# Gate vectors computed with tokens on the partitions, and an input norm with all token loads ahead and one scaling per tile

## The chip, the cores and the metric

The kernel runs on 1 core of one Trainium2 chip. The metric is the device time of one execution in microseconds (us). The kernel before took 2186.8, 2188.89 and 2193.44 us in three runs, median 2188.89 us.

A core has five engines with their own instruction streams: TensorE (PE in the profile, with its weight loads as PEld), VectorE (DVE), ScalarE (ACT), GpSimd (POOL) and SyncE (SP), which here only starts DMAs. Each engine works through its stream in order and waits on semaphores that other engines and DMAs raise.

## The reference, cut to what matters

The program is one inference step of a two-layer trunk: a gated DeltaNet layer and an RWKV-7 layer, over 8 x 8 sample tokens, 16 learned meta tokens and 1024 prompt tokens, 1104 rows of 1024 values in all. The change touches the start of the first layer: the RMSNorm of its input, and two small vectors for each token and each of 16 heads, `beta` and `g`, with the running sums of `g` that the chunked delta rule needs.

```python
def rmsnorm(x, w):
    xf = x.astype(jnp.float32)
    return xf * lax.rsqrt(jnp.mean(xf * xf, -1, keepdims=True) + RMS_EPS) * w.astype(jnp.float32)
...
proj = xn @ w_in
qkv, z, b, a = proj[..., :c1], proj[..., c1:c2], proj[..., c2:c3], proj[..., c3:]
beta = jax.nn.sigmoid(b)
g = -jnp.exp(a_log.astype(jnp.float32)) * jax.nn.softplus(a + dt_bias)
...
gc = jnp.cumsum(g, axis=-1)                      # within a chunk
decay = jnp.exp(jnp.where(causal, gc[..., :, None] - gc[..., None, :], -jnp.inf))
g_last = gc[..., -1]
k_dec = k * jnp.exp(g_last[..., None] - gc)[..., None]
q_dec = q * jnp.exp(gc)[..., None]
S = S * jnp.exp(gl_c)[..., None, None] + ...
```

The kernel cuts the 1104 rows into 9 token tiles: tile 0 holds the 64 sample tokens (8 chunks of 8 rows), the 16 meta tokens and 48 prompt tokens, tiles 1 to 7 hold 128 prompt tokens each and tile 8 the last 80. So the running sums restart every 8 rows in the first 64, at row 64, and at the start of every tile after that.

## The kernel before, in words

**Input.** `input_load` (L272) makes one tile `x` of 128 tokens by 1024 values for each of the 9 token tiles and loads it through SP's queue; tile 0 comes in three pieces, and the norm's weight is loaded once as `nwb`, the same row on all partitions. `build` (L2116) calls it for tiles 0 to 2 first; `layer0` (L2132) calls `gates_open`, which issues the loads of the gate weights `wz` (two DMAs of 16 columns out of a wide matrix) and of the two per-head constants `al`, and after it `input_load` for tiles 3 to 8.

`input_norm` (L280) works in groups of tiles, [0,1], [2,3,4], [5,6], [7,8]. For each tile ACT squares it with a running sum (`junk`, `ss`); then DVE, POOL (a power of -0.5, L103) and DVE (a Newton step, L111 to L113) turn the sums of a group into `rs`. Six of the tiles are scaled by `rs` and `nwb` in one DVE instruction (L299). The other three, 3, 5 and 7, are multiplied by `nwb` on POOL (L291) and by `rs` on ACT. Then PE transposes the tile in two halves of four 128x128 blocks into PSUM tiles named `r` (three buffers) and `f` (two buffers), ACT copies each half rounded to `xh` (tiles `xa`, `xc`), and DVE stores what was rounded off as `xl` (three instructions for each token tile, L313). Every later product of the layer uses the pair.

**Gates.** `gates_open` (L317) and the generator `gates` (L346) keep heads on the partitions and tokens along the free dimension: 16 partitions of 1104 tokens. `gates` projects with 64 columns of weights (three products named `d`, of 24 matmuls each, one for each segment of 384, 384 and 336 tokens), takes tanh, adds the bias, takes exp for each segment, then on all 1104 tokens at once log (ACT), max and add (L370), a multiply (L371), a running sum with restarts (L373, the one scan), and differences to the end of the chunk (L379 to L382). ACT takes the exp of the chunk ends (`egl`), which goes out to DRAM and comes back on all 128 partitions as `eglb`; the running sums themselves go to DRAM as `drow` in eight DMAs. Then nine PE transposes of 96 rows of `rows` give a form with tokens on the partitions, from which DVE and ACT fill `gcol`: beta, minus the sum, exp of the sum, exp of the distance to the end.

**Order.** From `layer0`'s products on, the order on PE and ACT is written by hand: each product of 128 output columns (`k`, `q`, `v`, `w`) takes six slots of 12 matmuls each, numbered from -24, and `gdn_events` (L921) puts other steps at fractions of slots; the five stages of `gates` stand at -22.9, -19.4, -16.8, -16.7 and -16.6 (L928). A product's PSUM tile is `dk`, `dq` or `dv`; its weights come as `wraw`, are split by ACT (`whi`, L87) and POOL (`wlo`, L91), half a product at a time. On DVE, POOL and SP, and on all engines in what lies ahead of the products, a list scheduler sets the order.

**What follows the gates.** For key head pair 0, `decays` (L643) reads `drow` back on all partitions as `E`, POOL masks it, ACT takes exps with `gcol` as bias, PE forms key scores `fsc`, DVE scales them (L700 to L710), they pass through DRAM to a blocked form `invA`, DVE inverts 72 triangular blocks in 31 dependent steps (L571, L573), and the result returns through DRAM as `T1n`, which PE's merges (`rY`) read. `history_turn` (L477) is one transpose, `mhist`, just ahead of the products' main part.

## Time and profile before

| | |
|---|---|
| runs | 2186.8, 2188.89, 2193.44 us; median 2188.89 us |
| the profiled execution's own time | 2190.08 us |
| its span, first to last instruction | 2188.3 us |
| granted TensorE clock, mean | 0.981 |
| PE busy | 2048.3 us, 94% |
| DVE busy | 1585.8 us, 72% |
| ACT busy | 1290.9 us, 59% |
| POOL busy | 841.2 us, 38% |

A row of the timeline reads: start, duration, engine, line, operation, output <- inputs, count, and in brackets how long the engine had been idle ahead of it and what released it. A row of the windows reads: the stretch, its length, then busy time and count for PE, PEld, DVE, ACT and POOL, the granted clock, the DMA engines' busy share, and GB/s. Matmuls overlap in the pipe, so what counts is the distance from one start to the next. SPq is SyncE's queue of DMA issues.

### The profile page before, as it was taken

To read this page: it belongs to the slowest core of one execution; us is meant where nothing else is said; L and a number is where in the kernel's file an instruction comes from. 1 tells how busy PE (TensorE), PEld (TensorE's weight loads), DVE (VectorE), ACT (ScalarE), POOL (GpSimd) and SP (SyncE) were. 2 spreads that over 40 slices of the span, in tenths; PEclk is the share of its full clock that TensorE was granted. 3 is DMA by queue.
4 is the path that set the end of the run, shared out by engine and by line. 5 is a ranking of instruction groups with operands and counts; after the bars stand their busy time and mean duration, and the time that the engine had idled before them with its cause. 6 is when DMAs were issued, how large, how long until landed. Compare 5 with 4: busy or idle time off the path is not lost. (4 is left out here: it accounts for less than half of the span.)

```text
span 2188.3 us, 54818 instructions
## 1 busy us (share of the span) xinstructions
PE 2048.3 (94%) x20404; PEld 1905.8 (87%) x20404; DVE 1585.8 (72%) x4221; ACT 1290.9 (59%) x3761; POOL 841.2 (38%) x1125
## 2 busy tenths in 40 slices
PE   5869899999999999999999999999898999999997
PEld 5859899999999999998899999888898988888876
DVE  7967869788887979795334676757968657777755
ACT  5526466656565665656533365664746446777774
POOL 3423333334343333334231352343534344444444
PEclk9979999999999999999999999999999999999999
DMA  4423342424333333335345115655565476677764
GB/s 119 119 58 87 90 115 85 116 78 106 96 96 106 105 96 102 98 102 165 97 126 134 61 51 190 215 167 168 168 180 152 119 221 175 181 229 221 239 178 138
DMA packets 430661, 292.65 MB, mean 134 GB/s; under 512 B 147145, under 2 KB 412986, under 8 KB 430394
## 3 DMA queue, kind: packets, MB, share of 16 engines
q1 hardware_dynamic: 430394, 289.14, 46.0%
q8 instruction: 161, 2.64, 0.5%
q14 instruction: 106, 0.87, 0.1%
HBM read 197.68 MB, written 91.37 MB: 132 GB/s over the span
## 5 line engine op out<-in xcount | busy, mean ns | idle before, releaser
L91 POOL TENSOR_TENSOR wlo<-wraw,whi 128x512 fp32r<-128x512 f32 (+1 forms) x246 | 328.5, 1337 | 475.8 <-ACT whi L87 432.1
L77 PE MATMUL d<-xc,whi 128*128 128x384 f32 (+2 forms) x1006 | 279.1, 336 | 0.8 <-DVE xc L313 0.7
L524 DVE SCALAR_TENSOR_TENSOR cvy<-raw,cw,cvy 128x408 f32<-128x408 f32 (+2 forms) x288 | 189.1, 657 | 19.2 <-ACT cvy L63 17.8
L87 ACT CAST whi<-wraw 128x512 fp32r<-128x512 f32 (+1 forms) x246 | 149.9, 612 | 87.2 <-PE d L77 50.0
L77 PEld LDWEIGHTS d<-xc,whi 128*128 128x128 f32 (+1 forms) x1006 | 183.0, 189 | 3.4 <-DVE xc L313 1.1
L77 PE MATMUL d<-xc,wlo 128*128 128x384 f32 (+3 forms) x476 | 157.5, 339 | 3.8 <-POOL wlo L91 3.8
L77 PE MATMUL dz<-xc,whi 128*128 128x384 f32 (+1 forms) x480 | 153.7, 338 | 0.0
L77 PE MATMUL dv<-xc,whi 128*128 128x384 f32 (+1 forms) x480 | 152.2, 337 | 0.0
L77 PE MATMUL d<-xa,whi 128*128 128x384 f32 (+3 forms) x450 | 142.9, 341 | 8.4 <-ACT ev L2352 4.1
L63 ACT ACTIVATE o<-rA,gcol 128x128 f32<-128x128 f32 x128 | 42.2, 367 | 116.2 <-DVE S L903 116.0
L571 DVE TENSOR_TENSOR invtmp<-invA,invT 72x31 f32<-72x31 f32 (+15 forms) x248 | 101.8, 411 | 3.2
L77 PE MATMUL dv<-xa,whi 128*128 128x384 f32 (+1 forms) x288 | 99.0, 344 | 0.0
L77 PE MATMUL dz<-xa,whi 128*128 128x384 f32 (+1 forms) x288 | 98.5, 342 | 0.0
L77 PEld LDWEIGHTS d<-xc,wlo 128*128 128x128 f32 (+1 forms) x476 | 89.2, 189 | 7.9 <-POOL wlo L91 4.9
L77 PEld LDWEIGHTS d<-xa,whi 128*128 128x128 f32 (+1 forms) x450 | 84.3, 190 | 12.9 <-ACT ev L2352 4.4
L573 DVE TENSOR_TENSOR invT<-invT,invtmp 72x31 f32<-72x31 f32 (+15 forms) x248 | 92.7, 374 | 3.3
L77 PEld LDWEIGHTS dz<-xc,whi 128*128 128x128 f32 x480 | 89.3, 188 | 4.6 <-issue 4.5
L77 PEld LDWEIGHTS dv<-xc,whi 128*128 128x128 f32 x480 | 89.1, 188 | 1.4 <-issue 1.4
L77 PE MATMUL d<-xa,wlo 128*128 128x384 f32 (+3 forms) x252 | 84.8, 337 | 2.0 <-POOL wlo L91 2.0
L77 PE MATMUL dq<-xc,whi 128*128 128x384 f32 (+1 forms) x240 | 78.3, 343 | 3.0 <-ACT whi L87 3.0
L77 PE MATMUL dk<-xc,whi 128*128 128x384 f32 (+1 forms) x240 | 78.2, 346 | 0.0
L1333 DVE SCALAR_TENSOR_TENSOR mixs<-xb,pcol,mixs 128x320 f32<-128x320 f32 (+2 forms) x96 | 69.4, 733 | 5.0 <-ACT mixs L63 4.7
(523 smaller groups left out, 6821.9 us busy)
## 6 DMA issues: line engine op xcount, KB each, us to landing
wraw<-in_gdn_w_in SPq DMA_DIRECT2D x96, 256.0 KB
wraw<-in_rwkv_w_rkvz SPq DMA_DIRECT2D x80, 256.0 KB
Sb<-in_state_gdn SPq DMA_DIRECT2D x64, 256.0 KB
sldcak<-cakd SPq DMA_DIRECT2D x24, 576.0 KB
wraw<-in_rwkv_w_o SPq DMA_DIRECT2D x42, 256.0 KB
E<-drow SPq DMA_DIRECT2D x24, 384.0 KB
attn<-drow SPq DMA_DIRECT2D x24, 384.0 KB
wraw<-in_gdn_w_out SPq DMA_DIRECT2D x36, 256.0 KB
```

Source lines behind the costliest of these rows:

```text
L63: return self.nc.scalar.activation(out, in_, func, bias=bias, scale=scale, **kw)
L77: self.nc.tensor.matmul(out, lhsT, rhs, start=start, stop=stop)
L87: nc.scalar.copy(hi, x)
L91: e.tensor_tensor(lo, x, hi.bitcast(F32), op=ALU.subtract)
L524: nc.vector.scalar_tensor_tensor(y[0][:, 0:wd], raw[:, k:k + wd], cw[k], y[0][:, 0:wd], op0=ALU.mult, op1=ALU.add)
L571: nc.vector.tensor_tensor(tmp, A[:, j, j + 1:32].unsqueeze(2).broadcast_to([nb, n, m]), Tv[:, j, 0:m].unsqueeze(1).broadcast_to([nb, n, m] ...
L573: nc.vector.tensor_tensor(Tv[:, j + 1:32, 0:m], Tv[:, j + 1:32, 0:m], tmp, op=ALU.subtract)
L1333: nc.vector.scalar_tensor_tensor(x[:, f:], xb[:, 8 + a + f:8 + b], mu, x[:, f:], op0=ALU.mult, op1=ALU.add)
```

## The change

Four things change.

1. `layer0` calls `input_load` for tiles 3 to 8 ahead of `gates_open`.
2. `input_norm` scales all nine tiles in one DVE instruction each; the POOL multiply and the ACT scaling are gone. The second half of tiles 2, 5 and 8 is transposed into PSUM tile `m` and no longer into `f`, and the transposes are issued at high priority.
3. The gates put tokens on the partitions. Each segment's product is copied to `rows` (48 partitions) by one ACT instruction; nine transposes of 48 rows bring everything into one PSUM tile `fgt`; from there on each instruction works on 128 partitions of 9 x 16 values. The running sums, the distances to the chunk's end, and the chunk ends on all partitions are products of PE with 0/1 masks (`upto`, `past`, `part`, built by POOL at the start), into `fgc` and `mge`; the scan, the differences and the DRAM round trip of `eglb` are gone. Two transposes (`fgr`) bring the sums back to rows for `drow`, whose layout stays, in two DMAs in place of eight.
4. The five stages of `gates` become four, at -23.4, -21.4 and -20.4 after the first.

The diff, cut:

```diff
@@ -287,23 +287,19 @@
...
-                if q not in (0,1,2,4,6,8):
-                    nc.gpsimd.tensor_tensor(x[0:nr], x[0:nr], self.nwb[0:nr], op=ALU.mult)
             nc.vector.tensor_scalar(ss, ss, 1.0 / D, RMS_EPS, op0=ALU.mult, op1=ALU.add)
             rs = t(lp, [128, len(qs)], "rs", 2)
             self.rsqrt(rs, ss, lp, "rn")
             for u, q in enumerate(qs):
                 x, nr = self.xrows[q]
                 r = rs[0:nr, u:u + 1]
-                if q in (0,1,2,4,6,8):
-                    nc.vector.scalar_tensor_tensor(x[0:nr], x[0:nr], r, self.nwb[0:nr], op0=ALU.mult, op1=ALU.mult)
-                else:
-                    self.act(x[0:nr], x[0:nr], AF.Identity, scale=r)
+                nc.vector.scalar_tensor_tensor(x[0:nr], x[0:nr], r, self.nwb[0:nr], op0=ALU.mult, op1=ALU.mult)
...
                 for h in (0, 1):
-                    p = self.ps("f", 2) if h else self.ps("r", 3)
-                    for k in range(4):
-                        self.transpose(p[:, 128 * k:128 * k + nr], x[0:nr, 512 * h + 128 * k:512 * h + 128 * k + 128])
+                    p = (self.ps("m", 1) if q % 3 == 2 else self.ps("f", 2)) if h else self.ps("r", 3)
+                    with self.tc.high_priority():
+                        for k in range(4):
+                            self.transpose(p[:, 128 * k:128 * k + nr], x[0:nr, 512 * h + 128 * k:512 * h + 128 * k + 128])
...
@@ -315,93 +311,99 @@
     def gates_open(self, ctx):
...
         gp = self.gatep = ctx.enter_context(self.tc.tile_pool(name="gates", bufs=1, reuse_waits="tile"))
...
-        al = t(gp, [128, 2], "al")
+        al = t(gp, [128, 2, 16], "al")
         wz = t(gp, [128, 8, 64], "wz")
...
         nc.sync.dma_start(wz[:, :, 0:16], wv[:, :, 0:16])
         nc.sync.dma_start(wz[:, :, 32:48], wv[:, :, 16:32])
-        rows = t(gp, [96, 1152], "rows")
...
-        nc.sync.dma_start(al[32:48, 0:1], i["gdn_a_log"].rearrange("l h -> h l"))
-        nc.sync.dma_start(al[32:48, 1:2], i["gdn_dt_bias"].rearrange("l h -> h l"))
+        for x, nm in enumerate(("gdn_a_log", "gdn_dt_bias")):
+            nc.sync.dma_start(al[:, x], i[nm].broadcast_to([128, 16]))
+        rows = t(gp, [48, 1152], "rows")
+        nc.gpsimd.memset(rows[:, NT:1152], NEG)
+        upto, past = [t(gp, [128, 128], f"upto{k}") for k in (0, 1)], [t(gp, [128, 128], f"past{k}") for k in (0, 1)]
+        for k in (0, 1):
+            for m, c, b in ((upto[k], 1, 0), (past[k], -1, -1)):
+                nc.gpsimd.memset(m, 1.0)
+                nc.gpsimd.affine_select(m, m, pattern=[[c, 128]], compare_op=ALU.is_ge, fill=0.0, base=b, channel_multiplier=-c)
+        nc.gpsimd.memset(upto[0][0:64, 64:128], 0.0)
+        nc.gpsimd.memset(past[0][64:128, 0:64], 0.0)
+        part = t(gp, [128, 9], "part")
+        nc.gpsimd.memset(part, 0.0)
+        nc.gpsimd.tensor_copy(part[0:64, 0:8], self.bmask[0:64])
+        nc.gpsimd.memset(part[64:128, 8:9], 1.0)
+        for m, c, b in ((upto[0], 1, 0), (past[0], -1, 7)):
+            v = m[0:64, 0:64].rearrange("p (b r) -> p b r", r=8)
+            nc.gpsimd.affine_select(v, v, pattern=[[-8 * c, 8], [0, 8]], compare_op=ALU.is_ge, fill=0.0, base=b, channel_multiplier=c)
+        self.gate_in = al, wz, rows, upto, past, part
     def gates(self, xh, xl):
         nc, i, t, gp = self.nc, self.i, self.t, self.gatep
-        al, wz, rows, g, sm = self.gate_in
-        nea = t(gp, [128, 1], "nea")
-        self.act(nea[32:48], al[32:48, 0:1], AF.Exp)
-        nc.vector.tensor_scalar(nea[32:48], nea[32:48], -1.0, None, op0=ALU.mult)
+        al, wz, rows, upto, past, part = self.gate_in
+        nea = t(gp, [128, 16], "nea")
+        self.act(nea, al[:, 0], AF.Exp)
+        nc.vector.tensor_scalar(nea, nea, -1.0, None, op0=ALU.mult)
...
         for s, (c0, n) in enumerate(SEGS):
             p = self.dense(w, 64, xh, xl, s)
-            b = rows[0:16, c0:c0 + n]
-            self.act(b, p[0:16, 0:n], AF.Tanh, scale=0.5)
-            nc.vector.tensor_scalar(b, b, 0.5, 0.5, op0=ALU.mult, op1=ALU.add)
...
-            self.act(xa, p[32:48, 0:n], AF.Identity, bias=al[32:48, 1:2])
-            nc.vector.scalar_tensor_tensor(ya, xa, -1.0, xa, op0=ALU.mult, op1=ALU.max)
-            self.act(ya, ya, AF.Exp, scale=-1.0)
+            nc.scalar.copy(rows[:, c0:c0 + n], p[0:48, 0:n])
         yield
...
-        self.act(ya, ya, AF.Ln, bias=1.0)
-        nc.vector.scalar_tensor_tensor(ya, xa, 0.0, ya, op0=ALU.max, op1=ALU.add)
-        nc.vector.tensor_scalar(g[32:48, 0:NT], ya, nea[32:48], None, op0=ALU.mult)
-        gc = rows[32:48]
-        nc.vector.tensor_tensor_scan(gc, sm[32:48], g[32:48], 0.0, op0=ALU.mult, op1=ALU.add)
+        col = self.col
+        p = self.ps("f", 2, "gt")
+        for k in range(9):
+            self.transpose(p[:, 48 * k:48 * k + 48], rows[:, 128 * k:128 * k + 128])
+        pv = p[:, 0:432].rearrange("p (k x) -> p k x", x=48)
+        b, x, y, g = [t(gp, [128, 9, 16], n) for n in ("gb", "gx", "gy", "g")]
+        nc.vector.tensor_tensor(x, pv[:, :, 32:48], al[:, 1].unsqueeze(1).broadcast_to([128, 9, 16]), op=ALU.add)
+        nc.vector.scalar_tensor_tensor(y, x, -1.0, x, op0=ALU.mult, op1=ALU.max)
+        self.act(y, y, AF.Exp, scale=-1.0)
+        self.act(b, pv[:, :, 0:16], AF.Tanh, scale=0.5)
+        self.act(y, y, AF.Ln, bias=1.0)
+        nc.vector.scalar_tensor_tensor(y, x, 0.0, y, op0=ALU.max, op1=ALU.add)
+        nc.vector.tensor_tensor(g, y, nea.unsqueeze(1).broadcast_to([128, 9, 16]), op=ALU.mult)
+        gs = t(gp, [128, 9, 16], "gs")
+        nc.vector.tensor_tensor(gs, g[:, 0].unsqueeze(1).broadcast_to([128, 9, 16]), part.unsqueeze(2).broadcast_to([128, 9, 16]), op=ALU.mult)
+        nc.vector.tensor_scalar(col[:, :, 0, :], b, 0.5, 0.5, op0=ALU.mult, op1=ALU.add)
         yield
...
-        nc.vector.tensor_tensor(c3(gd)[:, 1:9], v[:, 1:9, 127:128].broadcast_to([16, 8, 128]), v[:, 1:9], op=ALU.subtract)
...
-        nc.vector.tensor_tensor(c8(gd), v8[:, :, 7:8].broadcast_to([16, 8, 8]), v8, op=ALU.subtract)
-        egl = t(gp, [48, 17], "egl")
...
-        nc.sync.dma_start(dgl, egl[32:48])
...
+        flat = lambda a: a.rearrange("p k h -> p (k h)")
+        p = self.ps("f", 2, "gc")
+        for a, m in ((0, upto), (144, past)):
+            self.mm(p[:, a:a + 16], m[0], g[:, 0])
+            self.mm(p[:, a + 16:a + 144], m[1], flat(g[:, 1:9]))
+        c, d = (p[:, a:a + 144].rearrange("p (k h) -> p k h", h=16) for a in (0, 144))
+        gc = t(gp, [128, 144], "gc")
+        nc.vector.tensor_copy(gc.rearrange("p (j k h) -> p k j h", j=8, h=2), c.rearrange("p k (j h) -> p k j h", h=2))
+        e = self.ps("m", 1, "ge")
+        self.mm(e[:, 0:144], self.ones, flat(gs))
+        self.mm(e[:, 144:272], self.ones, flat(g[:, 1:9]))
+        self.act(col[:, :, 1, :], c, AF.Identity, scale=-1.0)
+        self.act(self.eglb.rearrange("p h c -> p c h"), e[:, 0:272].rearrange("p (c h) -> p c h", h=16), AF.Exp)
+        self.act(col[:, :, 2, :], c, AF.Exp)
+        self.act(col[:, :, 3, :], d, AF.Exp)
+        yield
+        p = self.ps("f", 2, "gr")
+        self.transpose(p[:, 0:128], gc[:, 0:128])
+        self.transpose(p[0:16, 128:256], gc[:, 128:144])
+        r = t(gp, [128, 256], "gr")
+        nc.vector.tensor_copy(r[:, 0:128], p[:, 0:128])
+        nc.vector.tensor_copy(r[0:16, 128:256], p[0:16, 128:256])
         self.drow = self.dram([8, 9, 2, 128], "drow")
-        for j in range(8):
-            nc.sync.dma_start(self.drow[j].rearrange("t h k -> h t k"), c3(gc)[2 * j:2 * j + 2])
-        for t3 in range(3):
-            yield
-            p = self.ps("f", 2)
-            for k in range(3):
-                self.transpose(p[:, 96 * k:96 * k + 96], rows[:, (3 * t3 + k) * 128:(3 * t3 + k + 1) * 128])
-            pv = p[:, 0:288].rearrange("p (k x h) -> p k x h", k=3, h=16)
-            c = self.col[:, 3 * t3:3 * t3 + 3]
-            nc.vector.tensor_copy(c[:, :, 0, :], pv[:, :, 0, :])
-            nc.vector.tensor_scalar(c[:, :, 1, :], pv[:, :, 2, :], -1.0, None, op0=ALU.mult)
-            self.act(c[:, :, 2, :], pv[:, :, 2, :], AF.Exp)
-            self.act(c[:, :, 3, :], pv[:, :, 4, :], AF.Exp)
+        d = self.drow.rearrange("j t h k -> (j t h) k")
+        nc.sync.dma_start(d[0:128], r[:, 0:128])
+        nc.sync.dma_start(d[128:144], r[0:16, 128:256])
...
@@ -925,7 +927,7 @@
...
-        for u in (-22.9, -19.4, -16.8, -16.7, -16.6):
+        for u in (-23.4, -21.4, -20.4):
             self.at(u, gate)
...
@@ -2138,8 +2140,8 @@
...
         self.gdn_keep(ctx)
         gates = ExitStack()
+        self.input_load(range(3, 9))
         self.gates_open(gates)
-        self.input_load(range(3, 9))
         self.input_norm(hi, lo)
...
```

How the order moves. First **SP's queue** at the program's start: `x_3`, `x_4` and the later `x` are token tiles, `wz` the gate weights, `al` the two constants, `wraw` the first key weights. Before:

```order
L278 DMA nwb_62<-in_norm_w 128x1024
L264 DMA x_3_64<-in_x_prompt 128x1024
L264 DMA x_4_66<-in_x_prompt 128x1024
L332 DMA wz_132<-in_gdn_w_in 128x8x16
L333 DMA wz_132<-in_gdn_w_in 128x8x16
L343 DMA al_131<-in_gdn_a_log 16x1
L344 DMA al_131<-in_gdn_dt_bias 16x1
L264 DMA x_23_146<-in_x_prompt 128x1024
L264 DMA x_24_148<-in_x_prompt 128x1024
```

After:

```order
L264 DMA x_4_66<-in_x_prompt 128x1024
L264 DMA x_15_123<-in_x_prompt 128x1024
L264 DMA x_16_125<-in_x_prompt 128x1024
L264 DMA x_17_127<-in_x_prompt 128x1024
L264 DMA x_18_129<-in_x_prompt 128x1024
L264 DMA x_19_131<-in_x_prompt 128x1024
L264 DMA x_20_133<-in_x_prompt 80x1024
L327 DMA wz_144<-in_gdn_w_in 128x8x16
L328 DMA wz_144<-in_gdn_w_in 128x8x16
L330 DMA al_143<-in_gdn_a_log 128x16
L330 DMA al_143<-in_gdn_dt_bias 128x16
L428 DMA wraw_371<-in_gdn_w_in 128x4x128
```

The six token tiles pass ahead of the gate weights and constants, and the constants come as 128 rows of 16 values.

Second, **DVE** between the end of the input norm and the first key rows: `cvy` is the key product's convolution, `rows`, `ay`, `g` the old gates on 16 partitions, the names with `g` behind them the new ones. Before:

```order
L370 SCALAR_TENSOR_TENSOR ay_413<-ax_412,ay_413 16x1104
L524 SCALAR_TENSOR_TENSOR cvy_565<-raw_524,cw_393,cvy_565 128x408
L371 TENSOR_SCALAR g_138<-ay_413,nea_405 16x1104
L373 SCALAR_TENSOR_TENSOR rows_136<-sm_140,g_138 16x1152
L524 SCALAR_TENSOR_TENSOR cvy_602<-raw_570,cw_393,cvy_602 128x384
L379 TENSOR_TENSOR rows_136<-rows_136 16x1024
L380 TENSOR_TENSOR rows_136<-rows_136 16x64
```

After:

```order
L370 TENSOR_TENSOR gx_554<-fgt_543,al_143 128x144
L371 SCALAR_TENSOR_TENSOR gy_555<-gx_554 128x144
L379 TENSOR_SCALAR gcol_135<-gb_553 128x9x16
L375 SCALAR_TENSOR_TENSOR gy_555<-gx_554,gy_555 128x144
L376 TENSOR_TENSOR g_556<-gy_555,nea_416 128x144
L378 TENSOR_TENSOR gs_564<-g_556,part_166 128x144
L526 SCALAR_TENSOR_TENSOR cvy_582<-raw_521,cw_404,cvy_582 128x408 x3
L388 COPY gc_611<-fgc_606 128x9x8x2
L401 COPY gr_641<-fgr_638 128x128
L402 COPY gr_641<-fgr_638 16x128
```

The gate steps now stand in one block ahead of the convolution, and each has 144 values to a partition, not 1104.

Third, **PE** in the key and query products: before, the gate transposes (`rows`) stand between the first and the second segment of the query product `dq`:

```order
L77 MATMUL dq_699<-xc_107,whi_626 128x384
L74 MATMUL f_726<-ident_74,rows_136 128x96 x3
L74 MATMUL f_734<-ident_74,rows_136 128x96 x3
L74 MATMUL f_742<-ident_74,rows_136 128x96 x3
L77 MATMUL dq_762<-xa_103,whi_585 128x384
```

After, the transposes `fgt` stand around `mhist`, and the mask products in the middle of the second key segment:

```order
L77 MATMUL d_475<-xc_107,whi_86_419 64x336
L74 MATMUL mhist_506<-ident_74,hist_501 128x96
L74 MATMUL fgt_543<-ident_74,rows_150 128x48 x3
L77 MATMUL dk_524<-xc_107,whi_379 128x384
L77 MATMUL dk_524<-xc_107,wlo_380 128x384
```

```order
L77 MATMUL dk_589<-xc_107,whi_375 128x384
L77 MATMUL fgc_606<-g_556,upto_27_152 128x16
L77 MATMUL fgc_606<-g_556,upto_28_153 128x128
L77 MATMUL fgc_606<-g_556,past_29_154 128x16
L77 MATMUL fgc_606<-g_556,past_30_155 128x128
L77 MATMUL mge_613<-gs_564,ones_82 128x144
L77 MATMUL mge_613<-g_556,ones_82 128x128
L77 MATMUL dk_589<-xc_107,whi_379 128x384
```

The two transposes `fgr` follow 12 matmuls later, at the end of that segment. The order on PE from the second query segment on is unchanged.

More of the change, by code (lines that the diff above doesn't have):

```diff
@@ L317, in gates_open @@
     def gates_open(self, ctx):
-        nc, i = self.nc, self.i
+        nc, i, t = self.nc, self.i, self.t
         W = i["gdn_w_in"][0]
-        self.col = self.t(self.l0, [128, 9, 4, 16], "gcol")
-        self.eglb = self.t(self.l0, [128, 16, 17], "eglb")
-        self.bmask4 = self.t(self.l0, [64, 4], "bmask4")
+        self.col = t(self.l0, [128, 9, 4, 16], "gcol")
+        self.eglb = t(self.l0, [128, 16, 17], "eglb")
+        self.bmask4 = t(self.l0, [64, 4], "bmask4")
         for g in (0, 1):
@@ L385, in gates @@
-        self.act(egl[32:48, 8:17].unsqueeze(2), v[:, :, 127:128], AF.Exp)
-        dgl = self.dram([16, 17], "dgl")
-        nc.sync.dma_start(dgl, egl[32:48])
-        nc.sync.dma_start(self.eglb.rearrange("p h c -> p (h c)"),
-                          dgl.rearrange("(o h) c -> o (h c)", o=1).broadcast_to([128, 272]))
-        self.drow = self.dram([8, 9, 2, 128], "drow")
-        for j in range(8):
-            nc.sync.dma_start(self.drow[j].rearrange("t h k -> h t k"), c3(gc)[2 * j:2 * j + 2])
```

20 lines of the change are left out of this document (removed).

## The prediction

> **What bounds the kernel now.** I began with the page's busy shares and then cut the span into windows, because the change touches only the first 75 us or so. PE is busy 94% of the span, and the 40 slices of the page show the first slice and a few others as the gaps. The windows around the start:
>
> ```profile
> 61.80:71.86 10.06, 5.84 (x22) 4.99 (x22) 9.19 (x19) 3.91 (x13) 3.60 (x9) 0.66 0.43 102
> 71.86:118.00 46.14, 43.83 (x321) 41.62 (x319) 44.14 (x127) 25.07 (x71) 22.05 (x37) 1.00 0.43 119
> 118.00:141.30 23.30, 2.96 (x18) 2.72 (x18) 18.04 (x47) 2.82 (x10) 4.39 (x5) 0.66 0.19 47
> 141.30:2188.00 2046.70, 1956.28 (x19813) 1822.05 (x19813) 1469.72 (x3956) 1222.92 (x3607) 788.84 (x1036) 0.99 0.47 136
> ```
>
> From 71.86 to 118 DVE is busy 44.1 of 46.1 us, and from 118 to 141.3 PE does next to nothing. The PE timeline names what it waits for:
>
> ```profile
> 141.32 0.31 PE L77 MATMUL rY<-T1n,E 32*32 32x32 f32 x2 [20.04 <-DMA T1n<-g_t]
> ```
>
> T1n is the end of one chain: gates, decays, key scores, then 31 dependent inversion steps on DVE, then DRAM. So up to 141 us the end is set by when DVE can begin the scores, not by PE's own work, and after it PE is busy 1956 of 2047 us in an order that the change leaves alone. Time won ahead of the scores passes through the 20 us wait to the end one for one; time won on PE alone, with T1n no earlier, would vanish in that wait. I therefore price the change at one point: the start of the second query segment on PE, 71.86 us, after which PE's order is the same and the scores follow at once.
>
> **What stands ahead of 71.86.** PE's rows in the query product:
>
> ```profile
> 61.46 0.33 PE L77 MATMUL dq<-xa,wlo 128*128 128x384 f32 x1
> 61.63 0.34 PE L77 MATMUL dq<-xc,whi 128*128 128x384 f32 x1
> 64.99 0.69 PE L77 MATMUL dq<-xc,whi 128*128 128x384 f32 x1 [3.02 <-ACT whi L87]
> ...
> 70.11 1.05 PE L74 MATMUL f<-ident,rows 96*128 96x96 f32 x6
> 71.61 0.47 PE L74 MATMUL f<-ident,rows 96*128 96x96 f32 x3 [0.46 <-ACT gcol L63]
> 71.86 0.42 PE L77 MATMUL dq<-xa,whi 128*128 128x384 f32 x1
> ```
>
> Starts are 0.17 us apart at full pace. After the 3.02 us wait the last 12 matmuls of the segment take from 64.99 to 70.11, 5.1 us where 12 x 0.175 = 2.1 would do, at a granted clock of 0.66 in that window. The weights `whi` were late because ACT, in order, sat on a convolution that DVE had not finished:
>
> ```profile
> 63.89 0.54 ACT L63 ACTIVATE raw<-cvy 128x408 f32<-128x408 f32 x1 [4.74 <-DVE cvy L524]
> ```
>
> and DVE had not finished it because the old gates stand between its taps:
>
> ```profile
> 55.63 1.30 DVE L370 SCALAR_TENSOR_TENSOR ay<-ax,ay 16x1104 f32<-16x1104 f32 x1 [3.61 <-ACT ay L63]
> 56.96 1.62 DVE L524 SCALAR_TENSOR_TENSOR cvy<-raw,cw,cvy 128x408 f32<-128x408 f32 x1
> 58.62 0.78 DVE L371 TENSOR_SCALAR g<-ay,nea 16x1104 f32<-16x1104 f32 x1
> 59.43 0.64 DVE L524 SCALAR_TENSOR_TENSOR cvy<-raw,cw,cvy 128x408 f32<-128x408 f32 x1
> 60.10 2.55 DVE L373 TENSOR_TENSOR_SCAN rows<-sm,g 16x1152 f32<-16x1152 f32 x1
> ```
>
> **Part 1, the gates: 5.4 us won.** I count from the transpose `mhist`, which stands near the same place in both orders.
>
> ```profile
> 50.29 0.25 PE L74 MATMUL mhist<-ident,hist 96*128 96x96 f32 x1
> ```
>
> Before, `mhist` to 71.86 is 21.6 us. After, PE has behind `mhist`: the wait for the third segment's copy to `rows` (0.45, as ACT's old copies, which were 16 wide, took 0.44 to 0.48) and three `fgt` transposes (0.35); 60 key matmuls, 36 x 0.175 + 24 x 0.155 = 10.0; six mask products; two `fgr` transposes, 0.2; 24 query matmuls, 4.2. The old kernel ran nothing like the mask products; the nearest row is
>
> ```profile
> 74.04 0.83 PE L77 MATMUL fsc<-K 128*128 128x128 f32 x6
> ```
>
> 0.14 each, so 0.7 for four full and two narrow ones (0.3 to 0.9 as bounds, all at a few tenths). With `mhist` itself that is 16.2 us; 21.6 - 16.2 = 5.4. It is the removed stall and slow stretch (6.8) less some more PE work (1.4).
>
> This holds only if no new stall comes. PE reaches the mask products 24 key matmuls, 4.2 us, behind the last `fgt`. In that time DVE must do four small steps, ACT two, with a table load between:
>
> ```profile
> 53.08 1.28 ACT L63 ACT_TABLE_LOAD   x1
> 54.38 1.22 ACT L63 ACTIVATE ay<-ay,cvals 16x1104 f32<-16x1104 f32 x1
> ```
>
> Steps of 144 values are not in the trace; `y`'s old step of 1104 values took 1.30 (L370 above) and steps of two or three values 0.16 (L112 below), so about 0.3 each, and 0.1 for each hand-over: 4 x 0.3 + 3 x 0.3 on ACT + 1.28 + 0.3 = 3.7 us, against 4.2. From below it is 3.0, from above, with 0.5 for each of the seven, 5.1: a stall between nothing and 0.9. I take none. The cover is the key product itself. In the trace the activation behind the load starts 0.02 us after it ends. The Trainium skill, ScalarE: Activation LUTs, section What ACT_TABLE_LOAD costs, puts about 1.38 us of drain on top of each load; by that the chain would be 5.1 us, PE would wait 0.9 and the sum would be 0.9 smaller. The two rows above show no such drain, so I stay with 3.7.
>
> The mask tiles on POOL (some 15 small memsets and selects at 0.1 to 0.3) end by about 7.5 us, ahead of POOL's first norm step, which needs the second square sum, so nothing. The eight `drow` DMAs and the `eglb` round trip leave SP; the two new DMAs leave at about 54, and `E` can be read back some two microseconds later. POOL's mask and DVE's use of `E` in the old trace:
>
> ```profile
> 71.14 0.87 POOL L651 TENSOR_SCALAR_AFFINE_SELECT E<-E 128x768 f32<-128x768 f32 x1
> ```
>
> ```profile
> 78.88 1.64 DVE L710 SCALAR_TENSOR_TENSOR E<-fsc,bp,E 128x128 f32<-128x128 f32 x6
> ```
>
> POOL had `E` by 71.1 and DVE needed it, after ACT's exps, at 78.9; those take some 3 us, so there are about 4 us of room, and `E` moves by about as much as PE. I cost it at nothing; if the room is used up, T1n is late one for one.
>
> **Part 2, the input norm and the load order: 3.8 us won at `mhist`.** SP spent 4.45 us on issuing one of the constants, so the fourth tile was issued at 11.4 and ACT waited for it:
>
> ```profile
> 6.45 4.45 SPq L343 DMA_DIRECT2D al<-in_gdn_a_log  x1
> ...
> 9.92 1.06 ACT L63 ACTIVATE junk<-x 128x1024 bf16<-128x1024 f32 x1 [1.33 <-DMA x<-in_x_prompt]
> ...
> 15.12 1.06 ACT L63 ACTIVATE junk<-x 128x1024 bf16<-128x1024 f32 x1 [1.75 <-DMA x<-in_x_prompt]
> ```
>
> In between, DVE and not the loads is the limit: it is busy nearly throughout 20 to 40 us. A piece of it:
>
> ```profile
> 19.71 2.30 DVE L111 TENSOR_TENSOR rn_t<-rs 128x3 f32<-128x3 f32 x1 [0.33 <-POOL rs L103]
> 22.05 0.16 DVE L112 SCALAR_TENSOR_TENSOR rn_t<-rn_t,ss 128x3 f32<-128x3 f32 x1
> 22.24 0.16 DVE L113 SCALAR_TENSOR_TENSOR rs<-rn_t,rs 128x3 f32<-128x3 f32 x1
> 22.44 2.48 DVE L299 SCALAR_TENSOR_TENSOR x<-x,rs,nwb 128x1024 f32<-128x1024 f32 x2
> 24.84 0.68 DVE L313 TENSOR_TENSOR xc<-r,xa 128x512 fp32r<-128x512 f32 x1
> 25.44 0.41 DVE L313 TENSOR_TENSOR xa<-f,xc 128x256 fp32r<-128x256 f32 x1
> 25.77 0.41 DVE L313 TENSOR_TENSOR xc<-f,xc 128x256 fp32r<-128x256 f32 x1
> ```
>
> L111 is a 0.16 us step; it took 2.30 because a POOL multiply ran beside it:
>
> ```profile
> L291 POOL TENSOR_TENSOR x<-x,nwb 128x1024 f32<-128x1024 f32 x3 | 7.1, 2372 | 1.1 <-ACT junk L63 1.1
> ```
>
> Two of the three multiplies cost DVE some 2.1 us each that way, the third 0.7: 5.0 in all, against three more scalings of 1.24 = 3.7. DVE's work from the first scaling on: nine scalings, 11.2; nine sets of three subtractions, from start to start 0.60 and 0.33 in these rows and 0.33 for the third, at 1.26 (the last tile less), 10.9; four groups of sums and Newton steps at 0.7, 2.8; the parameter columns, 0.7: 25.6. To this come 1.7 us without work while the second group's sums are made, and 2.5 where POOL's splits of the gate and key weights still run beside DVE. The first scaling comes at 11.5, since with the second tile no longer behind the gate weights ACT need not wait the 1.33 us. 11.5 + 25.6 + 1.7 + 2.5 = 41.3, against the old end of the last subtraction:
>
> ```profile
> 45.27 0.32 DVE L313 TENSOR_TENSOR xc<-f,xc 128x160 fp32r<-128x160 f32 x1
> ```
>
> 45.6, so DVE is 4.3 us earlier. PE's part behind the last transposes (the third gate segment, 12 key matmuls, eleven small transposes) is about 7.2 us, and puts `mhist` at about 46.5: 3.8 won. Bounds: if DVE gains nothing from POOL's absence and pays three scalings, -3.7; with no POOL beside it at all and no idle time, +7.
>
> **Part 3, the score steps: 0.8 won.** Before, ACT's copies into `gcol` stand just ahead of the query segment's first tap and delay it; the taps delay the first score on DVE. They are gone from there. Nothing to 1.8 us; I take 0.8.
>
> **The sum.** 5.4 + 3.8 + 0.8 = 10.0 us of the profiled execution's 2190.1, which gives 2180.1. The median of the three runs shown is 1.2 lower, so a median of 2179 to 2180; I say 2180. A measurement of this kernel can tell about 0.3% from no change, 6.6 us here.
>
> **The rivals.**
>
> *The norm gives nothing* (0.16). DVE is the limit there and gets 3.7 us more to do; if POOL's weight splits, which stay, cost it as much as the multiplies did, the front ends where it did or later. Then 5.4 - 3.7 to 5.4 + 0.8 remain: 2184 to 2188, about 2186, no change to speak of. For it: DVE's fullness. Against: 2.30 us for a 0.16 us step beside a multiply that goes.
>
> *PE waits for `g`* (0.09). If the chain of 3.7 is 3 us longer, PE stalls 3 us at the mask products and then pays a slow stretch like the one after 64.99, 3 us more: 10 - 6 = 4 won, 2186. The Trainium skill, TensorE: Matmul & The Clock Gate, part on the HAM clock gate, has the clock halve only after an idle window of about 3.4 us; by that a 3 us stall would cost itself alone, and this rival 2183. The old trace disagrees, with 0.66 granted around a wait of 3.02.
>
> *ACT blocked behind the gate weights* (0.07), the case that ends slower. ACT's cast of `wz` stands, in order, ahead of the last tile's squares and the casts of tiles 3 to 8, and `wz` is now loaded behind all tokens.
>
> ```profile
> 10.00:20.00 10.00, 3.91 (x16) 3.13 (x16) 6.83 (x12) 7.81 (x16) 6.28 (x6) 1.00 0.87 295
> ```
>
> ```profile
> 12.54 0.60 ACT L87 CAST whi<-wz 128x512 fp32r<-128x512 f32 x1
> ```
>
> Tokens and norm weight are 1104 + 128 rows of 4 KB, 5.05 MB; at 295 GB/s from 2 us on they are in by about 19. Behind eight tiles' squares ACT comes to the cast at about 20.5. The old `wz` was issued just ahead of the constants, at about 4, and cast at 12.54 without a wait, so it took at most 8.6 us: landed at 27.7 at worst, 7.2 lost, 2187. Each further microsecond passes straight on: from a landing at 30.5 it is slower than before, and at 42, 15 us later than the old row bears out, it would be 2201. Against it: nothing in the trace needs that long.
>
> *More is won* (0.13). No loss beside POOL and the full 1.8 of part 3: 13.5, 2176.5.
>
> The forecast keeps 0.55. Its own range is 2177 to 2184, from the bounds of its terms. The range 2174 to 2187 takes in the case above and the two without change. Faster by over 0.3%, below 2182.3: most of the forecast and the better case, 0.66; within: 0.27; slower: 0.07.
>
> **What would show it.** Right: no wait of PE between the key product and the second query segment, a granted clock near 1 there, that segment at about 62 us, T1n's wait still near 20 us and its end at about 131. Part 2 is wrong if `mhist` stands later than 48, part 1 if PE waits at `fgc`, part 3 if the first score step is not earlier against PE. If T1n moves by 10 and the end does not, the claim that the rest only shifts is wrong.

## The result, and the profile after

| | before | after |
|---|---|---|
| first comparison, median of 5 runs each | 2186.80 us | 2173.87 us |
| ratio of the runs, 95% interval | | 0.9943 [0.9924, 0.9962] |
| second comparison, median of 35 and 12 runs | 2182.81 us | 2173.86 us |
| ratio, 95% interval | | 0.9961 [0.9946, 0.9976] |
| profiled execution, its span | 2190.08, 2188.3 us | 2173.21, 2171.5 us |
| end of T1n's wait in two profiles each | 141.32, 142.87 us | 133.43, 134.30 us |

The changed kernel is faster by 12.5 us (8.3 to 16.6) in the first comparison and by 8.5 us (5.2 to 11.8) in the second; the prediction had 10.0. The changed median of 2173.87 lies 6.1 us below the 2180 that was forecast and 0.1 below the range of 2174 to 2187; 2.1 us of that are the kernel before, whose five runs have a median of 2186.80 where the forecast started from 2188.89. Single executions spread over 9 us (after) to 17 us (before) in the second comparison, so two profiles alone would mislead: the first two are 16.9 us apart.

PE's timeline of the changed kernel, from the history transpose to the second query segment; the columns are those of the rows before:

```profile
46.55 0.25 PE L74 MATMUL mhist<-ident,hist 96*128 96x96 f32 x1
47.23 0.38 PE L74 MATMUL fgt<-ident,rows 48*128 48x48 f32 x3 [0.44 <-ACT rows L362]
47.55 0.44 PE L77 MATMUL dk<-xc,whi 128*128 128x384 f32 x1
...
51.71 0.33 PE L77 MATMUL dk<-xc,whi 128*128 128x384 f32 x1
51.88 0.60 PE L77 MATMUL fgc<-g,upto 128*128 128x16 f32 x4
52.32 0.61 PE L77 MATMUL fgc<-g,past 128*128 128x16 f32 x4
52.77 0.41 PE L77 MATMUL mge<-gs,ones 128*128 128x144 f32 x2
53.01 0.38 PE L77 MATMUL mge<-g,ones 128*128 128x128 f32 x2
53.15 0.42 PE L77 MATMUL dk<-xc,whi 128*128 128x384 f32 x1
...
59.21 0.33 PE L77 MATMUL dq<-xa,whi 128*128 128x384 f32 x1
...
63.76 0.34 PE L77 MATMUL dq<-xa,whi 128*128 128x384 f32 x1
...
133.43 0.31 PE L77 MATMUL rY<-T1n,E 32*32 32x32 f32 x2 [20.05 <-DMA T1n<-g_t]
```

No row between 47.55 and 63.76 has a wait: the mask products start 0.17 us behind the matmul ahead of them, so `g` was there. The old stall of 3.02 us is gone. The windows of the changed kernel (length, then busy time of PE, PEld, DVE, ACT, POOL, the granted clock, DMA share, GB/s):

```profile
53.15:63.76 10.61, 10.54 (x65) 10.17 (x64) 7.23 (x14) 5.91 (x12) 4.46 (x9) 1.00 0.48 142
63.76:133.43 69.67, 46.91 (x338) 44.23 (x337) 63.48 (x173) 28.17 (x79) 30.03 (x43) 0.89 0.34 89
```

The granted clock, 0.66 in the query product before, is 1.00. From the second query segment to T1n the stretch lasts 69.7 us, before 141.32 - 71.86 = 69.5: up to T1n it moved as a block, with the same 20 us wait at its end.

### The profile page after: what moved, and what is told of

It reads as the page before. It is cut to its first block, busy times and chain, and to the rows that moved or that the text cites. A ratio compares the mean times of both kernels' runs of the same rounds, so it can differ in the third digit from the quotient of the medians.

```text
span 2171.5 us, 54811 instructions
## 1 busy us (share of the span) xinstructions
PE 2046.2 (94%) x20418; PEld 1905.8 (88%) x20418; DVE 1583.4 (73%) x4212; ACT 1283.1 (59%) x3750; POOL 834.9 (38%) x1136
## 5 line engine op out<-in xcount | busy, mean ns | idle before, releaser
L526 DVE SCALAR_TENSOR_TENSOR cvy<-raw,cw,cvy 128x408 f32<-128x408 f32 (+2 forms) x288 | 199.0, 692 | 17.1 <-ACT cvy L63 15.7
L77 PE MATMUL d<-xa,whi 128*128 128x384 f32 (+3 forms) x450 | 142.1, 340 | 4.5 <-ACT whi L87 1.7
```

The lines of the kernel that those rows point to most:

```text
L77: self.nc.tensor.matmul(out, lhsT, rhs, start=start, stop=stop)
L526: nc.vector.scalar_tensor_tensor(y[0][:, 0:wd], raw[:, k:k + wd], cw[k], y[0][:, 0:wd], op0=ALU.mult, op1=ALU.add)
```

## The experiments

Each kernel below was profiled once and timed in five rounds beside the kernel before. The lead at T1n is taken from the mean of the two profiles of before, 142.1; the lead in time is one minus the ratio, times the median of before in that comparison. L, N and G stand for the changed load order, norm and gates.

| kernel | mhist | second query segment | T1n's end | lead at T1n | ratio [95%] | lead in time, us |
|---|---|---|---|---|---|---|
| before | 50.29, 50.97 | 71.86, 72.55 | 141.32, 142.87 | | | |
| L (e1) | 53.94 | 75.07 | 144.36 | -2.3 | 1.0026 [1.0012, 1.0039] | -5.7 |
| L and N (e2) | 47.54 | 69.17 | 139.62 | 2.5 | 1.0000 [0.9988, 1.0013] | 0.0 |
| L and G (e3) | 54.00 | 71.20 | 141.26 | 0.8 | 0.9991 [0.9979, 1.0003] | 2.0 |
| G (e4) | 49.13 | 66.85 | 137.11 | 5.0 | 0.9978 [0.9966, 0.9990] | 4.8 |
| all again (e5) | 46.95 | 64.13 | 134.30 | 7.8 | 0.9961 [0.9946, 0.9976] | 8.5 |
| G and N (e6) | 47.21 | 65.61 | 134.89 | 7.2 | 0.9964 [0.9948, 0.9980] | 7.9 |
| N (e7) | 47.70 | 70.39 | 140.49 | 1.6 | 0.9999 [0.9984, 1.0015] | 0.2 |
| all, sum copied by ACT (e8) | 46.52 | 63.38 | 131.70 | 10.4 | 0.9955 [0.9938, 0.9971] | 9.8 |
| all, no priority (e9) | 46.77 | 64.42 | 133.57 | 8.5 | 0.9969 [0.9955, 0.9982] | 6.8 |
| all, POOL multiplies (e10) | 50.24 | 68.06 | 138.36 | 3.7 | 0.9994 [0.9982, 1.0006] | 1.3 |
| L and priority (e11) | 51.24 | 72.79 | 142.01 | 0.1 | 1.0020 [1.0005, 1.0034] | -4.4 |
| before again (e12) | 50.97 | 72.55 | 142.87 | | 0.9997 [0.9981, 1.0013] | 0.7 |

### The parts by themselves

The first question was why the first two profiles stand 16.9 us apart when T1n moved by 7.9. One theory was the order of layer 1: the scheduler swaps a few instructions there as a side effect of the change. The parts also carry one or the other order.

e1, the load order alone:

```diff
         gates = ExitStack()
-        self.gates_open(gates)
         self.input_load(range(3, 9))
+        self.gates_open(gates)
         self.input_norm(hi, lo)
```

> The kernel before with nothing but the token loads of tiles 3 to 8 put ahead of the gate weights and constants; norm and gates are the old ones. The start is limited by DVE and not by the loads, so both theories expect the chain T1n to end 0 to 1.5 us earlier than in the profile of before (141.3). They part behind it: the scheduler gives this kernel the same ACT order in layer 1 (the copies ev, the casts xh and whi) as the changed kernel. Theory A (the changed order in layer 1 wins some 5 us by itself): 4 to 7 us faster than before, and the lead over before grows between 1060 and 1700 us. Rival B (what the changed kernel won behind T1n is only the spread between two profiled executions): 0 to 1.5 us faster.

It was 5.7 us slower. That ends theory A as stated, and rival B as well: the load order costs something at the start. It gets the tokens in earlier, and so runs the POOL multiplies right beside the first DVE scalings. DVE in the profile of e1:

```profile
12.66 4.58 DVE L299 SCALAR_TENSOR_TENSOR x<-x,rs,nwb 128x1024 f32<-128x1024 f32 x2
...
18.31 2.30 DVE L111 TENSOR_TENSOR rn_t<-rs 128x3 f32<-128x3 f32 x1 [0.39 <-POOL rs L103]
...
36.27 1.28 DVE L299 SCALAR_TENSOR_TENSOR x<-x,rs,nwb 80x1024 f32<-80x1024 f32 x1
```

Two scalings take 4.58 us that took 3.50 in the kernel before and take 2.48 in the changed one (below). But the 3.0 to 3.7 us that `mhist` comes later are not lost there: the scaling of the last tile starts at 36.27, in the kernel before at 37.50. They are lost in PE's order. Transposes into `f` among the groups of PE up to 47 us, the kernel before and then e1 (busy time, mean ns of one, then the idle time ahead of them and what ended it):

```profile
L74 PE MATMUL f<-ident,x 128*128 128x128 f32 x32 | 6.2, 329 | 0.8 <-DVE xc L313 0.8
```

```profile
L74 PE MATMUL f<-ident,x 128*128 128x128 f32 x32 | 6.5, 348 | 5.3 <-DVE ss L292 5.3
```

In e1 four of these transposes stand ahead of all but one of the first gate product's matmuls and wait 5.3 us for DVE, up to 32.78. From 26 to 34 us PE is busy 2.67 us, in the kernel before 6.99, and the gate product follows at a granted clock of 0.77 (34 to 40 us, before 1.00).

e2 is the changed `input_norm` with e1's edit, e3 the changed gates with e1's edit, e4 the changed gates alone (their code as in the diff of the change, with the new stage numbers).

> The changed load order and input norm with the old gates, which keep their five stages. mhist is to stand at about 46.5 as in the changed kernel, the stall at whi stays (3 us at the query product), T1n ends about 3.7 us earlier than before, 137.6. The order in layer 1 is that of before. Theory A: 3 to 4.5 us faster than before in all. Rival B': the gain behind T1n comes with any earlier start (phase against DMAs), so it grows as in the changed kernel, by 12.9 to 7.9: about 6 us.

> The changed gates and load order with the old input norm (POOL multiplies and ACT scalings of tiles 3, 5 and 7). mhist stands at about 49 to 50.3 as before; from there to the second query segment 17.2 us as in the changed kernel against 21.6 before; T1n ends about 4.2 to 5 us earlier, 136.5 to 137. The order in layer 1 is that of before. Theory A: 4 to 5 us faster than before in all. Rival B': about 7 us.

> The changed gates alone, load order and norm as before. The constants now go out as 128 rows of 16 values ahead of the token tiles 3 to 8; if their issue takes less than the old 4.45 us on SP, mhist is up to 1 us earlier, else as before (50.3). From mhist to the second query segment 17.2 us; T1n ends 4 to 5 us earlier. The order in layer 1 is that of before. Theory A: 4 to 5 us faster in all. Rival B': about 7 us.

e4 did what was expected, 4.8 us in time and 4.2 against the first profile at T1n. e3 missed: the load order took back 4.9 us at `mhist` (54.00 against 49.13), and PE waits 4.68 us at the same transposes as in e1. e2 missed too: 2.8 to 3.4 us won at `mhist`, nothing in time. PE's waits in the query product, in the kernel before (behind the 3.02 us of 64.99) and then in e2:

```profile
66.42 0.69 PE L77 MATMUL dq<-xc,wlo 128*128 128x384 f32 x1 [0.74 <-POOL wlo L91]
```

```profile
61.73 0.44 PE L77 MATMUL dq<-xc,whi 128*128 128x384 f32 x1 [3.93 <-ACT whi L87]
63.54 0.69 PE L77 MATMUL dq<-xc,wlo 128*128 128x384 f32 x1 [1.38 <-POOL wlo L91]
```

PE comes to the query product earlier and waits there longer, 3.93 us and then 1.38 for the other half, where it was 3.02 and 0.74: the block of gate steps on DVE still holds the weights back. Even so the second query segment starts 2.7 to 3.4 us earlier and T1n ends 1.7 to 3.2 earlier, so the lead did not vanish on the way. Whether the time holds it cannot be told: its 0.0 us has an interval of -2.8 to 2.6.

### All again, and the two remaining pairs

e5 is the changed kernel unedited; e6 is the changed kernel with `gates_open` ahead of `input_load` as before; e7 is the changed `input_norm` alone.

> The changed kernel once more, unedited, beside the other parts on one chip. T1n is to end at about 133.4 again. Theory C (behind T1n everything only shifts, and the 12.5 us of the first comparison hold some 4 us of chance, five runs on either side): 7 to 9 us faster than before. Rival D (the changed order of layer 1 is worth 4 to 5 us where the start is early enough): 12 us or more.

> The changed gates and input norm with the load order of before (gate weights and constants ahead of tiles 3 to 8). Alone, the load order cost 3.0 us at T1n, and with the changed gates 4.2 (137.1 to 141.3). Theory E (it delays whatever norm stands behind it, by the gate weights' later cast on ACT): here T1n ends at 129.5 to 131, and the kernel is 2 to 4 us faster than the changed one. Rival F (it delays only the old norm, whose transposes stand behind the gate products on PE; the new norm issues them at high priority and needs the tokens early, since the fourth tile's squares come at 16.5 with the old order and at 13.1 with the new): T1n at 133.5 to 136, and the time that of the changed kernel or up to 3 us more.

> The changed input norm alone, with load order and gates as before. With both norm and load order, mhist stood at 47.5 and T1n ended at 139.6. Theory E: mhist at 45 to 46, T1n at 136 to 137.5, 4 to 5 us faster than before. Rival F: mhist 47.5 to 49, T1n 139.6 to 141.3, 0 to 2 us faster.

e5 came out at 8.5 us with T1n at 134.30: theory C. e6 has T1n 0.6 to 1.5 us later than the changed kernel and a time that cannot be told from it (rival F). e7 starts `mhist` at 47.70 and gains nothing measurable in time, as e2, though T1n ends 0.8 to 2.4 us earlier. In time the norm is worth 0.2 us alone (-3.3 to 3.5), and with the new gates 7.9 - 4.8, about 3 us, a difference of two leads that are each known to some 3 us. So it is not shown that the norm is worth more with the new gates: at T1n the leads of 5.0 and 1.6 add up to 6.6, and both together have 7.2.

e8 tests a wait that only shows behind the change. ACT in the changed kernel, behind the mask products:

```profile
51.63 0.60 ACT L87 CAST whi<-wraw 128x512 fp32r<-128x512 f32 x1
54.95 0.29 ACT L63 ACTIVATE gcol<-fgc 128x144 f32<-128x144 f32 x1 [2.72 <-DVE gc L388]
55.24 1.28 ACT L63 ACT_TABLE_LOAD   x1
56.54 0.66 ACT L63 ACTIVATE eglb<-mge 128x272 f32<-128x272 f32 x1
56.99 0.51 ACT L63 ACTIVATE gcol<-fgc 128x144 f32<-128x144 f32 x2
57.38 0.50 ACT L550 COPY raw<-dk 128x384 f32<-128x384 f32 x1
```

`fgc` was ready at about 53, but `gcol` starts at 54.95, released by `gc`, DVE's copy out of the same tile. Both only read it. The Trainium skill, PSUM — Partial Sum Buffer, section PSUM bank collisions raise a hardware error, says that the back end orders any two instructions of different engines on one bank and quadrant, reads included; the wait here agrees. Of its 2.72 us some 2.0 fall behind the moment when `fgc` was ready. `gc` stood on DVE behind three taps that began at 51.76. The edit:

```diff
-        nc.vector.tensor_copy(gc.rearrange("p (j k h) -> p k j h", j=8, h=2), c.rearrange("p k (j h) -> p k j h", h=2))
+        nc.scalar.copy(gc.rearrange("p (j k h) -> p k j h", j=8, h=2), c.rearrange("p k (j h) -> p k j h", h=2))
```

> The changed kernel with the copy gc of the running sums out of PSUM moved from DVE to ACT, nothing else. In the changed kernel's trace ACT is idle 2.7 us ahead of gcol and released by DVE's gc, which stands behind three taps that began 51.76. Theory G (this wait delays the key rows and so the scores): ACT starts gc at about 53.2, gcol at 53.6, the key segment's copy raw 1 to 1.3 us earlier than its 57.38, and T1n ends 0.5 to 1.3 us earlier, about 132.5. Rival H (DVE's taps beside POOL are the limit there): the copies come earlier, T1n stays within 0.3 of 133.4.

```profile
52.95 0.28 ACT L388 COPY gc<-fgc 128x144 f32<-128x144 f32 x1 [0.73 <-PE fgc L77]
53.12 0.30 ACT L63 ACTIVATE gcol<-fgc 128x144 f32<-128x144 f32 x1
...
55.55 0.50 ACT L550 COPY raw<-dk 128x384 f32<-128x384 f32 x1
```

The key segment's copy is 1.83 us earlier, more than the 1.0 to 1.3 expected, and T1n ends at 131.70, 1.7 to 2.6 us earlier: theory G. What is left of ACT's wait is 0.73 us, for `fgc` itself. In time the ratio is the best of all, but 0.9955 and 0.9961 cannot be told apart.

### What of the norm it is

e9 takes the priority away, e10 puts the POOL multiplies back into the changed kernel, e11 adds the priority to e1.

```diff
-                    with self.tc.high_priority():
-                        for k in range(4):
-                            self.transpose(...)
+                    for k in range(4):
+                        self.transpose(...)
```

> The changed kernel with the input norm's transposes issued at ordinary priority. The prediction gave the priority no term of its own. Theory F (the early token loads pay only because the priority keeps the transposes ahead of the gate products on PE): mhist at 49.5 to 51.5 in place of 46.6 to 47.0, T1n 3 to 4.5 us later (137 to 138), and 3 to 5 us slower than the changed kernel. Rival I (the norm's gain comes from DVE alone, scaling in one instruction with no POOL beside it): mhist at 46.5 to 47.5, T1n at 133.4 to 134.5, no difference in time.

```diff
                 self.act(junk[0:nr], x[0:nr], AF.Square, accum=ss[0:nr, u:u + 1])
+                if q not in (0,1,2,4,6,8):
+                    nc.gpsimd.tensor_tensor(x[0:nr], x[0:nr], self.nwb[0:nr], op=ALU.mult)
...
-                nc.vector.scalar_tensor_tensor(x[0:nr], x[0:nr], r, self.nwb[0:nr], op0=ALU.mult, op1=ALU.mult)
+                if q in (0,1,2,4,6,8):
+                    nc.vector.scalar_tensor_tensor(x[0:nr], x[0:nr], r, self.nwb[0:nr], op0=ALU.mult, op1=ALU.mult)
+                else:
+                    self.act(x[0:nr], x[0:nr], AF.Identity, scale=r)
```

> The changed kernel with tiles 3, 5 and 7 multiplied by nwb on POOL and scaled on ACT again as before; the rest of the changed norm (load order, tile m, priority) stays. The prediction's sum gave the three multiplies beside DVE 5.0 us and three more scalings on DVE 3.7: by it mhist is 1.3 us later, 47.9 to 48.3, and L111 takes 2.3 us again in two places. Rival J (the multiplies' ACT half also delays ACT's copies, so that more is lost): mhist at 49.5 or later, T1n 3 us later. Rival K (DVE has slack there): mhist within 0.5 of 46.6 to 47.0.

> The kernel before with the changed load order and the transposes at high priority; scaling on POOL and ACT, tile f and the gates as before. Theory F: the 3.7 us that the load order alone lost at mhist (53.9) are gone: mhist at 47.5 to 50, T1n at 139.5 to 141. Rival L (the loss came from the old norm's chain through POOL and ACT standing behind the cast of the gate weights): mhist still at 52 to 54, T1n at 143 to 144.5, 3 to 6 us slower than before.

e9 changes nothing at T1n (133.57) and nothing in time that can be told: rival I. It also carries the old order of layer 1, as e2, e3, e4 and e10 do, and gains 6.8 us (3.9 to 9.8), which speaks against rival D, as e5 did. e10 loses 3.3 to 3.7 us at `mhist`, 4.1 to 4.9 at T1n, and most of the gain in time (1.3 us are left, -1.3 to 3.9): rival J's size. Its reason, that ACT's scalings delay ACT's copies, was not tried by itself. DVE in e10:

```profile
13.82 4.59 DVE L299 SCALAR_TENSOR_TENSOR x<-x,rs,nwb 128x1024 f32<-128x1024 f32 x2
...
19.46 2.30 DVE L111 TENSOR_TENSOR rn_t<-rs 128x3 f32<-128x3 f32 x1 [0.98 <-POOL rs L103]
...
26.93 1.96 DVE L111 TENSOR_TENSOR rn_t<-rs 128x2 f32<-128x2 f32 x1
28.81 0.16 DVE L360 TENSOR_SCALAR nea<-nea 128x16 f32<-128x16 f32 x1
28.92 1.20 DVE L112 SCALAR_TENSOR_TENSOR rn_t<-rn_t,ss 128x2 f32<-128x2 f32 x1
30.16 1.19 DVE L113 SCALAR_TENSOR_TENSOR rs<-rn_t,rs 128x2 f32<-128x2 f32 x1
```

and the same steps in the changed kernel:

```profile
13.34 2.48 DVE L296 SCALAR_TENSOR_TENSOR x<-x,rs,nwb 128x1024 f32<-128x1024 f32 x2
15.74 0.16 DVE L290 TENSOR_SCALAR ss<-ss 128x3 f32<-128x3 f32 x1
16.88 0.16 DVE L111 TENSOR_TENSOR rn_t<-rs 128x3 f32<-128x3 f32 x1 [0.97 <-POOL rs L103]
...
25.70 1.32 DVE L111 TENSOR_TENSOR rn_t<-rs 128x2 f32<-128x2 f32 x1
```

Each multiply costs DVE about its own length: 4.59 - 2.48 = 2.1, 2.30 - 0.16 = 2.1, 1.96 - 0.16 = 1.8, together 6.0 against the steps by themselves. The third of them is not free in the changed kernel either: it takes 1.32 there, beside a weight split on POOL. L112 and L113 in e10 then lose another 1.0 each to the weight splits. The Trainium skill, SBUF — State Buffer, section Who interferes with whom, calls the port pair of the two engines an exclusive lock; a step of 0.16 us that lasts 2.30 beside a POOL multiply of 2.35 agrees.

e11 ends between its two theories, T1n at 142.01, and is 4.4 us slower than before. It shows what the load order cost at `mhist` in e1: its two rows on DVE are as long (4.59 and 2.29 us), but with the priority PE does the gate product ahead of those transposes, the wait of 5.3 us is gone, and `mhist` stands at 51.24, 0.3 to 1.0 behind the kernel before. So some 2.7 of the 3.0 to 3.7 us were PE's order and not the steps beside POOL.

### The kernel before once more

> The kernel before, unedited, as one of the two: what two samples and two profiles of one kernel differ by. Theory C (the start repeats, and what the profile of before lost behind 1060 us against all others is chance): T1n at 140.5 to 142, a span 4 to 14 us shorter than the 2188.3 of the first profile, the difference arising in layer 1 behind 1060 us; ratio 1 within its interval. Rival D (the order of layer 1 makes it): a course like the first profile's, within 3 us of it from 1060 to the end.

T1n ends at 142.87, 1.6 later than in the first profile, and the span is 2181.6, 6.7 shorter: 8.2 us of difference arise behind T1n between two executions of one program. Over all fourteen profiles the time behind T1n's wait lies between 2032 and 2047 us, and the first profile of before is the longest of them. Of two PE waits in the stretch 1035 to 1265, before in the first profile and then in this one (what waited and for what, us in total, how often, the longest):

```profile
PE f L74 <- DMA stage<-in_x_prompt: 4.7, 3, 1.9
PE frss L77 <- DVE rsum L1241: 3.1, 1, 3.1
```

```profile
PE f L74 <- DMA stage<-in_x_prompt: 3.1, 4, 1.1
PE frss L77 <- DVE rsum L1241: 1.9, 1, 1.9
```

These two account for 2.8 of the 8.2 us; they differ here between two executions of the same kernel. T1n itself was 1.6 later where the expectation allowed 142, so a single profile holds its place to some 1.5 us.

## Why the prediction came out as it did

The step from 71.86 to T1n was right: the block moved as one. From T1n to the end the single profiles spread too far to say, and the times have to. For e2 to e10 the lead at T1n lies in the interval of the lead in time. e1 misses it by 0.3 us and e11 by 1.2: both are slower in time than their one profile says at T1n, and that stays open. The gain of 10.0 at T1n was 7.8 and 8.7 in the two profiles of the changed kernel, and 7.9 between the two of the first comparison. The interval in time of that comparison, 8.3 to 16.6, takes in the 8.7 and just misses the 7.9. At the second query segment the terms, 10.0 in sum, came to 8.1: two of the three were too large, and the number of the third was right by luck. That 10.0 lies between the measured 8.5 and 12.5 owes something to chance as well, since their intervals are 7 to 8 us wide:

**Part 1, the gates: 5.4 predicted, 4.4 measured** from `mhist` to the second query segment (21.57 before, 63.76 - 46.55 = 17.21 after, 17.18 in e5). The mechanism was right: the stall and the slow stretch went, no wait came in their place, the chain from `fgt` to `g` took some 3.7 us as worked out, and the activations behind the table loads started 0.01 and 0.02 us after them, with no drain (48.86 + 1.28 to 50.15, the load within that chain, and 55.24 + 1.28 to 56.54). Too small was the added work on PE. From 47.55 to 59.21 are 11.66 us where the sum had 10.0 + 0.7 + 0.2 = 10.9: the mask products alone take 53.15 - 51.88 = 1.27 where 0.7 was put. The rows show why: the six products are 12 matmuls (x4, x4, x2, x2), two for each, and the sum had priced six at one row's 0.14. The query segment took 4.55, not 4.2.

**Part 2, norm and load order: 3.8 predicted at `mhist`, 3.74 measured (3.3 to 4.4 over two profiles each).** The number was right and its account was not. The first scaling was to come at 11.5, since ACT would not wait for the second tile once it was no longer behind the gate weights. It had never been behind them, as SP's rows of the kernel before show:

```profile
3.00 0.91 SPq L264 DMA_DIRECT2D x<-in_x_prompt  x2
3.95 0.43 SPq L332 DMA_DIRECT2D wz<-in_gdn_w_in  x1
```

In the changed kernel ACT waited longer, and the scaling came at 13.34:

```profile
10.55 1.06 ACT L63 ACTIVATE junk<-x 128x1024 bf16<-128x1024 f32 x1 [2.01 <-DMA x<-in_x_prompt]
```

The load order is not what sets this wait: it is 1.05 to 2.59 us in the nine profiles with the new order and 1.33 to 2.25 in the five with the old one. The start was 1.8 us late, DVE's work behind it took 27.9 us where the sum had 29.8, and its last subtraction ended at 41.20, forecast 41.3: two errors that cancel. Two things made the loss good. POOL's absence is worth more than the 5.0 - 3.7 = 1.3 of the sum: e10, without it, is 3.3 to 3.7 later. And part of the lead belongs to the gates: with them alone (e4) `mhist` is already at 49.13, 1.2 to 1.8 earlier. The old gates had steps in the front too (L362 and L365 took 1.5 us of DVE at 43.48, ahead of the last subtractions), which is the likely reason. The load order, named with the norm, contributes at most 0.3 to 0.7 at `mhist` beside the new norm (e6) and harms the old one (e1, e3).

**Part 3, the score steps: 0.8 predicted, nothing measured.** The copies into `gcol` are gone from the old place, but ACT waits for `gc`, some 2.0 us longer than for `fgc` alone, and the key rows come late. DVE's scaling L710 (L712 in the changed kernel) leads by 78.88 - 70.77 = 8.11, no more than the query segment's 8.10. This step failed as put: it asked what leaves ACT's way and not what the new reads of one PSUM tile wait for. e8 removes that wait, and the lead at L710 is 78.88 - 68.91 = 9.97 against 71.86 - 63.38 = 8.48, so 1.5 from the step: within its bounds of nothing to 1.8.

**The rivals.** "The norm gives nothing" is not what the profiles show: alone it moves `mhist` by 2.6 to 3.3 us and T1n by 0.8 to 2.4 (e7), and on top of the new gates by 1.9 and 2.2 (e6 against e4). In time neither step is clear of the noise by itself. "PE waits for `g`" did not happen. "ACT blocked behind the gate weights" did not either: the changed kernel casts `wz` at 21.69 without a wait. "More is won", 13.5, lies inside the interval of the first comparison and above that of the second, 11.8, and T1n moved by less than 9; its reason, no loss beside POOL and the full 1.8 of part 3, did not come about. e8, with 1.5 of that 1.8, has 9.8 (6.3 to 13.5).

## What to carry to other kernels

A part that measures nothing alone may still be worth keeping: the norm by itself gives 0.2 us with 3.4 either way, while its marks in the profile, `mhist` and T1n, move by 1 to 3 us. Read such a part at the point where its effect must pass, and do not conclude from the times alone that parts fail to add. Price a POOL operation beside DVE at its own length on DVE, and an earlier load also by the order that the scheduler then makes of PE's work: in e1 a transpose that waits for its buffer held back a product that could have run. When two engines read one PSUM tile, look where each stands in its queue, since the later one waits for the earlier.

## What the runs showed of the hardware that was not expected

A DVE step of 0.16 us lasted 2.30 beside a 2.35 us POOL multiply, and the order of loads decided on which steps this fell: with tokens early, the two first scalings took 4.58 in place of 3.50. Two engines that only read one PSUM tile took turns in the order of the program, which left ACT idle some 2.0 us longer than its input asked for. The granted clock fell around short waits too: in e7 PE waits 1.98 and 1.37 us in the query product, and the clock is 0.50 from 64.75 to 70.39. And SP's issue of a DMA lasts about 4 us at some point between 6 and 20 us, whatever is issued there:

```profile
11.76 3.83 SPq L328 DMA_DIRECT2D wz<-in_gdn_w_in  x1
15.64 3.93 SPq L330 DMA_DIRECT2D al<-in_gdn_a_log  x1
```

In the kernel before it was the constant at 6.45, with 4.45 us, as one column of 16 rows; here the gate weights and the constant as 128 rows take nearly the same, and e4, with the constant as 128 rows in the old place, has 4.71 at 6.97. So the 4.45 were not the price of that constant's shape, and putting the tokens ahead moved the wait behind them.
